# First mixer: the low part of each weight goes to VectorE or to GpSimd as a clock kept at build time tells

## The chip, the core and the metric

The kernel runs on one NeuronCore of a Trainium2 chip. The core's engines run side by side, each with its own queue of instructions: TensorE (PE in the profile; its weight loads are shown apart as PEld), VectorE (DVE), ScalarE (ACT), GpSimd (POOL) and SyncE (SP), which here only issues transfers. The metric is the device time of one execution in microseconds (us).

## The reference

Two transformer blocks run one after the other on 256 tokens of width 2048, all in float32. The change is in the first mixer of the first block:

```python
proj = h @ w_in[l]                                   # 8208 columns
o_hg  = hgrn2_group(proj[..., :HG_COLS], ...)        # q, f, v, g: 8 heads of 128
o_gdn = gdn_group(proj[..., HG_COLS:], ...)          # q, k, v through a causal convolution, gate, a, b
y = jnp.concatenate([o_hg, o_gdn], axis=-1) @ w_out[l]
x = x + gt_m * rmsnorm(y, post_mix_norm[l])
...
mod = silu(c) @ w_ada + b_ada                        # the shifts, scales and gates of a block
```

`hgrn2_group` and `gdn_group` are recurrences over chunks. The kernel turns each into a chain of small matrix products, exponentials, masks and products of elements.

## The kernel before

**Weights.** Every large weight is read once. It comes in units of 512 KB (128 partitions x 1024 values, tile `raw`), which SyncE loads into one of five buffers. A float32 product is made of three faster ones, so ScalarE rounds a unit to its high part (`wh<-raw`), and another engine makes the low part, which is the unit less its high part (`wl<-raw,wh`). TensorE then multiplies with both (`g<-hT,wh`, `g<-hT,wl`, or `g<-wh,hT`, as the block is laid out). There are four pairs of `wh` and `wl`. A raw buffer comes free for the next transfer once both parts are made. The other users of raw buffers are the units of the modulation, which VectorE multiplies and adds up (`acc<-raw,csil,acc`).

**Who makes the low part.** `l_eng` decides: an item marked `low` 3 goes to GpSimd if the build-time clock has it finished there no more than 3 us later than on VectorE, one marked otherwise goes to GpSimd if the mark is true and to VectorE if it is 0. Before, no weight of the first mixer has a mark. Those of the second mixer have, and there GpSimd makes 88 low parts.

**The build-time clock.** While the program is written out, `clk` runs a model of every engine (1.042 ns an element for a VectorE product, 2.2 ns for one on GpSimd). Each engine has its own time in it, and nothing in it couples VectorE with GpSimd. The order of instructions on every engine follows from this clock, and on the chip each engine keeps that order.

**The first mixer.** Its products run in 512-column blocks: `hq`, `hf`, `hv`, `hg`, (`ab`), `zq`, `zk`, `zv`, `gg` for the first half of the heads, and the same again for the second half; then `oA` and `oB`, the output projection. Three quarters of the first half's products run ahead of the stage. Between the products of a block, `fill` puts in steps of the chains, and makes the next units ready. The chains are generators (`hg_gen` of L1074, `gd_gen` of L1131, `head_out` of L1045):

- `hg_gen` has seven levels. On each, TensorE multiplies `hq,hk`, VectorE copies under a mask into `hgA` (COPY_PREDICATED) and updates `hq` and `hf`, and GpSimd updates `hk`. `head_out` then scales (`hgA<-hgA,rr,hg`), TensorE turns the result (`mx<-c,hgA`), and GpSimd makes its low part (`ol`). There are two of those, one for each half of the tokens.
- `gd_gen` inverts a triangular matrix in six levels. On each, TensorE multiplies `gdP,gdE`, ScalarE copies to `gdG`, TensorE multiplies `gdG,gdT`, VectorE subtracts from `gdP`, TensorE turns `gdP`. GpSimd masks `gdE`.
- The convolution (`zq`, `zk`, `zv`) is three multiply-adds of VectorE for each head. In the first half they read `part`, which is in SBUF; in the second half they read `g`, which is in PSUM.

Where a block's own follow-up is not done, the next one may not begin. `run` (L570) then takes steps of the chains, whichever the clock puts first, with no products between them:

```python
        while len(pri) > 1:
            clk.end = 0.0
            pri_step()
            if not clk.end:
                fill_step(True)
```

The case that matters is `hv` of the second half. Ahead of it, `ev_q` (L936) of the second half waits for the end of the first half's `hg_gen`:

```python
            while half and g.get("hg_done") != 0:
                yield
```

All engine instructions go through one helper, so the profile shows them under line 169; they are told apart by their tiles.

Of the kernel before, what the change touches and what calls it, by code (L numbers as in the profile page):

```python
# [178 lines left out]
def two_blocks(ctx, tc, I, out):  # L179
# [3 lines left out]
    pe, dve, act, pool, sync = (_Eng(clk, n, e) for n, e in (  # L183
        ("pe", nc.tensor), ("dve", nc.vector), ("act", nc.scalar), ("pool", nc.gpsimd), ("sync", nc.sync)))
# [45 lines left out]
    items = []  # L230
# [5 lines left out]
    def add_w(pieces, nk, n):  # L236
        items.append({"pieces": pieces, "nk": nk, "n": n})
        return len(items) - 1

    def add_ada(blk, vq, k, fin, row, cg):  # L240
        items.append({"ada": (blk, vq, k), "fin": fin, "row": row, "cg": cg})
# [46 lines left out]
    def prep(low=None):  # L288
# [14 lines left out]
        if "ada" in it:  # L303
            blk, vq, k = it["ada"]
            if it["cg"]:
                return ada_cg(it)
            a = st["accs", blk, vq]
            sc = csil[:, blk * 16 + k:blk * 16 + k + 1]
            if k == 0 and not it["row"]:
                dve.tensor_scalar(a, it["raw"], sc, None, op0=MUL)  # L310
            else:
                dve.scalar_tensor_tensor(a, it["raw"], sc, a, op0=MUL, op1=ADD)
            if it["fin"]:
                it["fin"]()
        else:
            n_ = it["nk"] * it["n"]
            it["slot"] = k, p = slots.popleft()
            h = p.tile([128, UK * 512], FR, name="wh", tag=f"wh{k}")
            l = p.tile([128, UK * 512], FR, name="wl", tag=f"wl{k}")
            act.activation(h[:, :n_], it["raw"][:, :n_], AF.Copy)  # L320
            if low is None:
                low = l_eng(it)
            low.tensor_tensor(l[:, :n_], it["raw"][:, :n_], h[:, :n_], op=SUB)
            held[k] = clk.key(h), clk.key(l)
            it["pe"] = 6 * n_ * 0.42e-3
            st["ahead"] += it["pe"]
            it["h"] = h[:, :n_].rearrange("p (k n) -> p k n", k=it["nk"])
            it["l"] = l[:, :n_].rearrange("p (k n) -> p k n", k=it["nk"])
# [36 lines left out]
    held = {}  # L365

    def l_eng(it):
        if it.get("low") != 3:
            return pool if it.get("low") else dve
        n = it["nk"] * it["n"]  # L370
        h = clk.t["act"]
        a = max(h, clk.t["dve"]) + 0.07 + n * 1.042e-3
        b = max(h, clk.t["pool"]) + 0.1 + n * 2.2e-3
        return pool if b <= a + 3.0 else dve

    def late_prep():
        i = st["p"]
        if i >= len(items) or "raw" not in items[i] or "ada" in items[i] or items[i].get("whole"):
            return False
        it = items[i]  # L380
        n = it["nk"] * it["n"]
        h = max(clk.t["act"], prep_at()) + 0.1 + n * 0.833e-3
        if it.get("low"):
            done = max(h, clk.t["pool"]) + 0.2 + n * 2.2e-3
        else:
            done = max(h, clk.t["dve"]) + 0.2 + n * 1.042e-3
        return done > clk.t["pe"] + st["ahead"] - lag[4]

    def prep_at():

        i = st["p"]
        if i >= len(items) or "raw" not in items[i]:
            return 0.0
        it = items[i]
        at = clk.wr[clk.key(it["raw"])][0]
        if "ada" not in it and slots:
            at = max([at] + [clk.rd.get(k, 0.0) for k in held.get(slots[0][0], ())])
        return at
# [57 lines left out]
    def fill(more=True):  # L456
        if pri:
            pri_step()
        fill_step(False, urgent)
        if more and late_prep():  # L460
            prep()
        for _ in range(2):
            if clk.t["dve"] - clk.t["pe"] > lag[1] or clk.t["act"] - clk.t["pe"] > lag[2] or not fill_step():
                break
        if more:
            for _ in range(2):
                if prep_at() > clk.t["pe"] + lag[3] or not prep():
                    break
# [1483 lines left out]
    def weight(k):  # L1952
        if k[0] in ("oB", "pB") or k == "fv" or k in (("f1", 0, 0), ("ga", 0, 0)) or k[:3] in (("f1", 0, 1), ("f2", 3, 2), ("f2", 3, 3)):
            return 0.0
        if k in ("qG", "kvH", "sv"):
            return 0.5
        if k == "ab" or k[1:] == (0,) and k[0] in ("hq", "hf", "hv", "hg", "zq", "zk", "zv", "gg"):
            return 0.0
        if k in (("hq", 1), ("hf", 1)):
            return 0.5  # L1960
        if k[0] == "oA":
            return 1.5
        return 1.0

    LOW = {k: 1 for k in ("qG", "kvH", "sv", "qA", "kB", "qC", "kD", "dv0", "dv1", "qE", "kF", "fdv")}
    LOW.update({k: 3 for k in LOW if isinstance(k, str)})
    for k in ("qG", "kvH"):
        del LOW[k]
    LOW.update({("pA", c): 2 for c in range(4)})
    ai = n_first  # L1970
    wide = [blocks[n, 0] for n in ("hq", "hf", "hv", "hg", "zq", "zk", "zv", "gg")]
    q_items = [ADA[q * 16:q * 16 + 16] for q in range(4)]
# [21 lines left out]
    for endkey, ntot in phases:  # L1994
        hi = order.index(endkey) + 1
        tot = sum(len(blocks[k].us) * weight(k) for k in order[lo:hi])
        tot = tot * 0.5 if endkey[0] == "up" else tot - (3 if endkey[0] == "pA" else 0 if endkey == "fdv" else 24)
        a0, na = ai, ntot - ai
        done = 0.0
        for k in order[lo:hi]:  # L2000
            b = blocks[k]
            b.idx = []
            for u in b.us:
                b.idx.append(add_w(*u))
                if k in (("f1", 0, 0), "fv", ("ga", 0, 0)):
                    items[-1]["whole"] = True
                items[-1]["low"] = k in LOW and (LOW[k] if LOW[k] == 3 else len(b.idx) % LOW[k] == 0)
                done += weight(k)
                while ai < ntot and (ai - a0) < na * done / tot:
                    for _ in range(1 + ADA[ai][5]):  # L2010
                        add_ada(*ADA[ai])
                        ai += 1
        lo = hi
# [65 lines left out]
    for b, o in zip(wide[1:], ("hk", "hv", "hg", "oh1", "ol1", "oh2", "ol2")):  # L2079
        a = g[o] if o in g else oTp.tile([128, 2, 512], F32, name="part", tag=o)  # L2080
# [140 lines left out]
    b = blocks["f2", 3, 3]  # L2221
# [97 lines left out]
    b = blocks["pB", 0]  # L2319
# [64 lines left out]
    b = blocks["dn", 2, 3]  # L2384
# [48 lines left out]
```

## Time and profile before

| what | value |
|---|---|
| time, median of 3 runs | 2723.72 us (2722.84 to 2728.7) |
| profiled execution: its own time | 2722.54 us |
| its span | 2720.8 us |
| TensorE busy | 2614.4 us (96%) |
| VectorE busy | 1823.5 us (67%) |
| ScalarE busy | 1261.0 us (46%) |
| GpSimd busy | 382.7 us (14%) |
| low parts on VectorE | 705, 871.2 us |
| low parts on GpSimd | 88, 206.0 us |

An engine's busy time is the sum of its instructions from start to end. An instruction that waits inside itself counts as busy for that long, so a busy share does not say how much work was done. Times below are counted from the start of the span. The first mixer, from where the second stage of its products begins, takes from 211 to about 740 us.

### The profile page before, as it was taken

What the parts mean: (1) busy time and instruction counts of PE and PEld (TensorE: products, weight loads), DVE (VectorE), ACT (ScalarE), POOL (GpSimd) and SP (SyncE); (2) the same over time, 40 slices, a digit from 0 to 9 for tenths busy, and PEclk for the clock granted to TensorE, in tenths of its full rate; (3) what the DMA queues carried; (4) which work ended last, traced back from release to release, by engine and by line L of the source; (5) the groups of instructions that cost most, each with busy time, mean ns of one, the idle gap of its engine ahead of it and who ended that gap; (6) DMA issues with size and microseconds to landing.
All of it is one profiled execution on the core that took longest, in us unless ns stands there. A gap on an engine that the chain in (4) does not pass through costs nothing.

```text
span 2720.8 us, 39596 instructions
## 1 busy us (share of the span) xinstructions
PE 2614.4 (96%) x15073; PEld 2198.1 (81%) x15073; DVE 1823.5 (67%) x2259; ACT 1261.0 (46%) x2124; POOL 382.7 (14%) x250
## 2 busy tenths in 40 slices
PE   7999889899999999999999999898999999999998
PEld 4788869768778888888886898796778888888886
DVE  3567978954678787887855465568767656655566
ACT  3434444344554454544544355454454444443443
POOL 1001142231000000000001155563400000000001
PEclk9999999999999999999999999998999999999999
DMA  9985968985579989989965865667677777666664
GB/s 361 318 262 148 239 194 219 264 251 184 174 252 302 319 284 303 318 291 325 311 192 165 233 205 179 210 220 243 212 232 244 244 244 219 196 191 192 188 186 147
DMA packets 399805, 643.58 MB, mean 237 GB/s; under 512 B 31480, under 2 KB 198088, under 8 KB 398208
## 3 DMA queue, kind: packets, MB, share of 16 engines
q1 hardware_dynamic: 391904, 627.03, 72.6%
q10 hardware_dynamic: 6960, 11.65, 1.2%
q8 instruction: 118, 1.93, 0.3%
q0 software_dynamic: 752, 2.39, 0.2%
q14 instruction: 71, 0.58, 0.1%
HBM read 636.27 MB, written 4.19 MB: 235 GB/s over the span
## 4 chain that ended last, share of the span: by engine, by line
PE 59%; DVE 4%; DMA 4%; issue 2%; ACT 2%; POOL 1%; SPq 0%; ACTq 0%; POOLq 0%; DVEq 0%
PE g L169 56%; PE mx L169 3%; DMA raw<-in_w_ff_dram 2%; DMA raw<-in_w_in_dram 1%; DVE wl L169 1%; ACT wh L169 1%; DVE acc L169 1%; DMA raw<-in_w_out_dram 1%; POOL wl L169 1%; DMA raw<-in_ada_w_dram 0%; DVE y L169 0%; DVE xres L169 0%; ACT S L169 0%; ACT sq L169 0%; DVE Sc L169 0%
## 5 line engine op out<-in xcount | busy, mean ns | idle before, releaser
L169 DVE TENSOR_TENSOR wl<-raw,wh 128x1024 fp32r<-128x1024 f32 x705 | 871.2, 1243 | 538.4 <-ACT wh L169 536.1
L169 ACT ACTIVATE wh<-raw 128x1024 fp32r<-128x1024 f32 (+2 forms) x793 | 823.5, 1045 | 880.1 <-PE g L169 391.7
L169 PE MATMUL g<-hT,wh 128*128 128x512 f32 (+1 forms) x4448 | 1212.1, 344 | 9.7 <-ACT wh L169 5.2
L169 PE MATMUL g<-hT,wl 128*128 128x256 f32 x3376 | 951.6, 282 | 8.7 <-DVE wl L169 5.8
L169 PEld LDWEIGHTS g<-hT,wh 128*128 128x128 f32 x4448 | 768.7, 190 | 125.5 <-issue 18.3
L169 PEld LDWEIGHTS g<-hT,wl 128*128 128x128 f32 x3376 | 641.4, 190 | 12.0 <-DVE wl L169 7.0
L169 DVE SCALAR_TENSOR_TENSOR acc<-raw,csil,acc 128x1024 f32<-128x1024 f32 x276 | 389.5, 1411 | 58.6 <-DMA raw<-in_ada_w_dram 57.4
L169 PE MATMUL g<-wh,rh 128*128 128x512 f32 x864 | 339.4, 393 | 0.0
L169 PE MATMUL g<-wh,rl 128*128 128x512 f32 x864 | 339.1, 393 | 0.0
L169 PE MATMUL g<-wl,rh 128*128 128x512 f32 x864 | 339.0, 392 | 0.0
L169 POOL TENSOR_TENSOR wl<-raw,wh 128x1024 fp32r<-128x1024 f32 (+2 forms) x88 | 206.0, 2354 | 232.5 <-ACT wh L169 218.8
L169 PEld LDWEIGHTS g<-wh,rh 128*128 128x128 f32 x864 | 162.6, 188 | 36.0
L169 PEld LDWEIGHTS g<-wh,rl 128*128 128x128 f32 x864 | 162.5, 188 | 36.1
L169 PEld LDWEIGHTS g<-wl,rh 128*128 128x128 f32 x864 | 162.7, 188 | 35.8
L169 PE MATMUL g<-wh,hT 128*128 128x512 f32 (+2 forms) x544 | 162.1, 369 | 2.1 <-ACT hq L169 1.8
L169 PEld LDWEIGHTS g<-wh,hT 128*128 128x128 f32 x544 | 97.9, 189 | 28.2 <-issue 12.6
L169 POOL TENSOR_TENSOR y<-yy,gw 128x512 f32<-128x512 f32 x6 | 7.7, 1301 | 697.2 <-DVE yy L169 697.2
L169 PE MATMUL g<-wl,hT 128*128 128x512 f32 (+2 forms) x272 | 98.4, 362 | 5.7 <-POOL wl L169 3.2
L169 PE MATMUL g<-raw,y 128*128 128x512 f32 (+1 forms) x192 | 84.2, 581 | 3.1 <-DVE y L169 2.9
L169 POOL TENSOR_TENSOR y<-y,gw 128x512 f32<-128x512 f32 x6 | 9.6, 1626 | 547.0 <-DVE y L169 541.5
L169 PE MATMUL ada<-raw,csil 128*32 128x512 f32 x384 | 63.8, 658 | 10.8 <-DMA raw<-in_w_ada_dram 9.3
L169 PEld LDWEIGHTS g<-raw,y 128*128 128x128 f32 x192 | 34.3, 190 | 38.1 <-issue 28.7
(453 smaller groups left out, 2569.7 us busy)
## 6 DMA issues: line engine op xcount, KB each, us to landing
raw<-in_w_ff_dram SPq DMA_DIRECT2D x256, 512.0 KB, 5.4
raw<-in_w_ada_dram SPq DMA_DIRECT2D x192, 512.0 KB, 5.7
raw<-in_ada_w_dram SPq DMA_DIRECT2D x192, 512.0 KB, 5.3
raw<-in_w_in_dram SPq DMA_DIRECT2D x176, 512.0 KB, 5.9
raw<-in_ffn_w_gate_dram SPq DMA_DIRECT2D x88, 512.0 KB, 4.6
raw<-in_ffn_w_up_dram SPq DMA_DIRECT2D x88, 512.0 KB, 4.7
raw<-in_ffn_w_down_dram SPq DMA_DIRECT2D x88, 512.0 KB, 4.4
raw<-in_w_out_dram SPq DMA_DIRECT2D x60, 512.0 KB, 4.8
```

Source lines behind the costliest of these rows:

```text
L169: r = f(out, *a, **kw)
```

## The change

Low parts of the first mixer get the mark 4: all blocks `hq` to `gg` from the point where the three early quarters are done, `ab`, and `oA`. Mark 4 means GpSimd if the build-time clock has it finished there no later than on VectorE, otherwise VectorE. `late_prep`, which decides whether a unit must be made ready at once, asks the same question. Nothing else is edited.

```diff
     def l_eng(it):
-        if it.get("low") != 3:
+        if it.get("low") not in (3, 4):
             return pool if it.get("low") else dve
         n = it["nk"] * it["n"]
         h = clk.t["act"]
         a = max(h, clk.t["dve"]) + 0.07 + n * 1.042e-3
         b = max(h, clk.t["pool"]) + 0.1 + n * 2.2e-3
-        return pool if b <= a + 3.0 else dve
+        return pool if b <= a + (3.0 if it["low"] == 3 else 0.0) else dve
...
-        if it.get("low"):
+        if it.get("low") and l_eng(it) is pool:
             done = max(h, clk.t["pool"]) + 0.2 + n * 2.2e-3
...
     LOW.update({("pA", c): 2 for c in range(4)})
+    LOW.update({(n, h): 4 for n in ("hq", "hf", "hv", "hg", "zq", "zk", "zv", "gg") for h in range(2)})
+    LOW.update({("oA", c): 4 for c in range(4)})
+    LOW["ab"] = 4
...
-                items[-1]["low"] = k in LOW and (LOW[k] if LOW[k] == 3 else len(b.idx) % LOW[k] == 0)
+                items[-1]["low"] = k in LOW and (LOW[k] if LOW[k] in (3, 4) else len(b.idx) % LOW[k] == 0)
```

In the program that comes out, GpSimd makes 118 low parts and VectorE 675, so 30 have moved. By their place among GpSimd's own instructions, 11 of them lie in the levels of the first `hg_gen` and its `head_out`, 2 in the first half's `gd_gen`, 12 in the second half's `hg_gen` and what stands beside it, and 5 in the second half's `gd_gen`. SyncE's order does not change.

On GpSimd, at the last levels of the first `hg_gen` (`hk` is the update of a level, `rr` and `ol` belong to `head_out`, `gdM` and `gdE` open `gd_gen`), the program before has:

```order
L169 TENSOR_TENSOR hk<-hk,hf 128x64x8
L169 TENSOR_TENSOR hk<-hk,hf 128x32x16
L169 TENSOR_TENSOR hk<-hk,hf 128x16x32
L169 TENSOR_TENSOR hk<-hk,hf 128x8x64
L169 TENSOR_TENSOR rr<-rr,mhalf 128x4
L169 TENSOR_TENSOR ol_3033<-hgA,oh_3032 128x4x128
L169 TENSOR_TENSOR rr<-rr,mhalf 128x4
L169 TENSOR_TENSOR ol_3033<-hgA,oh_3032 128x4x128
L169 TENSOR_TENSOR gdM_3309<-c_84,gla 128x512
```

and the changed one:

```order
L169 TENSOR_TENSOR hk<-hk,hf 128x64x8
L169 TENSOR_TENSOR wl<-raw,wh 128x1024 x2
L169 TENSOR_TENSOR hk<-hk,hf 128x32x16
L169 TENSOR_TENSOR wl<-raw,wh 128x1024
L169 TENSOR_TENSOR hk<-hk,hf 128x16x32
L169 TENSOR_TENSOR wl<-raw,wh 128x1024 x2
L169 TENSOR_TENSOR hk<-hk,hf 128x8x64
L169 TENSOR_TENSOR wl<-raw,wh 128x1024
L169 TENSOR_TENSOR rr<-rr,mhalf 128x4
L169 TENSOR_TENSOR wl<-raw,wh 128x1024 x3
L169 TENSOR_TENSOR ol_3006<-hgA,oh_3005 128x4x128
L169 TENSOR_TENSOR rr<-rr,mhalf 128x4
```

Nine of the eleven low parts of this place are in these rows (one stands ahead of them, one behind); `gdM` now comes after them.

On VectorE, at the last two of those levels, this is a piece of the difference:

```order
 L169 SCALAR_TENSOR_TENSOR acc<-raw,csil,acc 128x1024
-L169 TENSOR_TENSOR wl<-raw,wh 128x1024
 L169 COPY_PREDICATED hgA<-mk_1973,mx 128x4x64 x2
 L169 TENSOR_TENSOR hq<-hq,hf 128x8x64
 L169 TENSOR_TENSOR hf<-hf 128x8
 L169 SCALAR_TENSOR_TENSOR acc<-raw,csil,acc 128x1024
-L169 TENSOR_TENSOR wl<-raw,wh 128x1024
 L169 SCALAR_TENSOR_TENSOR zq<-part,cols,zq 128x253
```

The low parts are gone, and what stood around them stays. From the start of the stage to the second `hgA<-hgA,rr,hg`, VectorE has 23 low parts before and 13 after, and 13 and 14 `acc` steps.

On TensorE, where the products stop ahead of `hv` of the second half (`c_84` is the unit matrix, `g<-wh,hT` is the first product of `hv`), the program before has:

```order
L169 MATMUL mx<-c_84,hgA 128x128 x4
L169 MATMUL mx<-c_84,zk 128x128 x4
L169 MATMUL mx<-c_84,zq 128x128 x4
L169 MATMUL mx<-gdM_3309,c_84 128x512
L169 MATMUL mx<-gdE_3312,c_84 128x512
L169 MATMUL mx<-zk 128x128 x4
L169 MATMUL mx<-c_84,zk 128x128 x4
L169 MATMUL mx<-c_84,zv 128x128 x4
L169 MATMUL g<-wh,hT_176 128x512
```

and the changed one, from the turning of `zv` on (the rows ahead of it are the same but for `hgA`, which comes later):

```order
L169 MATMUL mx<-c_84,zv 128x128 x4
L169 MATMUL mx<-c_84,hgA 128x128 x4
L169 MATMUL mx<-c_84,gdT_3315 128x128 x4
L169 MATMUL mx<-gdP_3316,gdE_3317 128x64 x4
L169 MATMUL mx<-gdG_3312,gdT_3315 128x64 x4
L169 MATMUL mx<-c_84,gdP_3316 128x128 x4
L169 MATMUL mx<-gdP_3316,gdE_3317 128x64 x4
L169 MATMUL mx<-c_84,zq 128x128 x4
L169 MATMUL mx<-gdG_3312,gdT_3315 128x64 x4
L169 MATMUL mx<-c_84,gdP_3316 128x128 x4
L169 MATMUL mx<-gdP_3316,gdE_3317 128x64 x4
L169 MATMUL mx<-gdG_3312,gdT_3315 128x64 x4
```

Two more rows (`mx<-c_84,gdP` and `mx<-gdP,gdE`) follow before the first product of `hv`. So three levels of `gd_gen` and the start of a fourth, which before stood between products, now stand with no product between them.

## Rows read from the trace of the kernel before

**Rows 1.** Windows: us, busy PE, PEld, DVE, ACT, POOL; granted clock, DMA share, GB/s.

```profile
246.00:337.00 91.00, 83.03 (x663) 81.37 (x663) 86.99 (x140) 38.94 (x69) 18.18 (x10) 0.97 0.79 203
331.00:349.00 18.00, 9.03 (x35) 6.09 (x36) 9.37 (x20) 9.70 (x43) 11.66 (x10) 0.72 0.41 109
450.00:540.00 90.00, 79.92 (x638) 75.91 (x637) 84.04 (x123) 35.91 (x85) 23.06 (x16) 0.98 0.83 233
540.00:620.00 80.00, 73.53 (x444) 51.44 (x443) 39.84 (x71) 33.67 (x89) 29.22 (x24) 0.98 0.83 258
```

**Rows 2.** What TensorE waited for from 211 to 740 us.

```profile
PE g L169 <- DVE wl L169: 8.4, 7, 2.5
...
PE mx L169 <- DVE gdP L169: 4.0, 3, 2.1
```

**Rows 3.** VectorE's groups, 246 to 337: busy, mean ns | idle before.

```profile
L169 DVE TENSOR_TENSOR wl<-raw,wh 128x1024 fp32r<-128x1024 f32 x21 | 26.3, 1261 | 2.5 <-ACT wh L169 2.5
L169 DVE SCALAR_TENSOR_TENSOR acc<-raw,csil,acc 128x1024 f32<-128x1024 f32 x13 | 17.4, 1339 | 0.0
L169 DVE SCALAR_TENSOR_TENSOR zq<-part,cols,zq 128x255 f32<-128x255 f32 (+2 forms) x12 | 6.8, 564 | 0.3
L169 DVE COPY_PREDICATED hgA<-mk,mx 128x256 f32<-128x256 uint8 x14 | 6.6, 525 | 0.7 <-PE mx L169 0.6
L169 DVE TENSOR_TENSOR hq<-hq,hf 128x512 f32<-128x512 f32 x7 | 6.0, 856 | 0.0
L169 DVE SCALAR_TENSOR_TENSOR zv<-part,cols,zv 128x255 f32<-128x255 f32 (+2 forms) x12 | 5.7, 478 | 0.1
...
L169 DVE TENSOR_TENSOR part<-g,part 128x512 f32<-128x512 f32 x8 | 5.1, 679 | 0.0
```

**Rows 4.** VectorE's groups, 760 to 1480, where GpSimd is nearly idle.

```profile
L169 DVE TENSOR_TENSOR wl<-raw,wh 128x1024 fp32r<-128x1024 f32 x248 | 301.1, 1225 | 124.9 <-ACT wh L169 124.0
L169 DVE SCALAR_TENSOR_TENSOR acc<-raw,csil,acc 128x1024 f32<-128x1024 f32 x122 | 156.1, 1279 | 0.9 <-DMA raw<-in_ada_w_dram 0.4 <-DMA raw<-in_w_ada_dram 0.2
```

**Rows 5.** Instructions in time (start, length): VectorE and GpSimd, mostly second mixer.

```profile
306.08 0.68 DVE L169 TENSOR_TENSOR hq<-hq,hf 128x512 f32<-128x512 f32 x1
504.71 1.06 POOL L169 TENSOR_TENSOR hk<-hk,hf 128x512 f32<-128x512 f32 x1 [6.98 <-PE mx L169]
1606.01 2.39 POOL L169 TENSOR_TENSOR wl<-raw,wh 128x1024 fp32r<-128x1024 f32 x1 [1.76 <-ACT wh L169]
1606.18 2.37 DVE L169 TENSOR_TENSOR Sc<-Sc,cs 128x128 f32<-128x128 f32 x1
1608.78 0.29 DVE L169 TENSOR_TENSOR Sc<-Sc,cs 128x128 f32<-128x128 f32 x1
1610.90 2.37 POOL L169 TENSOR_TENSOR wl<-raw,wh 128x1024 fp32r<-128x1024 f32 x1 [2.50 <-ACT wh L169]
1611.77 1.95 DVE L169 SCALAR_TENSOR_TENSOR S<-cb,mx 128x384 f32<-128x384 f32 x4 [1.50 <-PE mx L169]
1616.68 1.94 DVE L169 SCALAR_TENSOR_TENSOR S<-cb,mx 128x384 f32<-128x384 f32 x4
```

**Rows 6.** TensorE in time around the stop ahead of `hv`.

```profile
336.07 1.17 PE L169 MATMUL mx<-c,hgA 128*128 128x128 f32 x4 [5.45 <-DVE hgA L169]
...
348.37 0.50 PE L169 MATMUL g<-wh,hT 128*128 128x512 f32 x1 [1.77 <-ACT hq L169]
...
357.73 0.50 PE L169 MATMUL g<-wl,hT 128*128 128x512 f32 x1 [2.50 <-DVE wl L169]
```

**Rows 7.** The steps of one level of `gd_gen`, in time.

```profile
408.36 1.00 PE L169 MATMUL mx<-gdP,gdE 128*128 128x64 f32 x8
409.46 0.39 ACT L169 ACTIVATE gdG<-mx 128x256 f32<-128x256 f32 x1 [0.30 <-PE mx L169]
410.15 0.41 DVE L169 TENSOR_TENSOR gdP<-gdP,mx 128x256 f32<-128x256 f32 x1
410.71 0.63 PE L169 MATMUL mx<-c,gdP 128*128 128x128 f32 x4
```

## The prediction

> **What bounds the kernel now.** I read the page first: TensorE is busy for 96% of the span, so outside the mixers there is little to win or to lose, and the change edits only the first mixer. Then the busy time by stretches, and the reader is to see where VectorE is full [rows 1]. From 246 to 337 it is busy for 86.99 of 91 us, from 450 to 540 for 84.04 of 90; from 540 to 620 for only 39.84 of 80. These full stretches are where it could be worth taking work off VectorE. Then TensorE's waits: from 211 to 740 it waits 8.4 us for low parts of VectorE and 4.0 us for `gdP` [rows 2]. In time, its longest wait is 5.45 us, for the scaled `hgA` of VectorE, at 336.07, where all products of the first half are done and those of `hv` may not begin before 348.37 [rows 6]. VectorE is thus what this stretch waits for at its end: whatever makes VectorE later at 336 makes TensorE later by as much. GpSimd is far from full there (18.18 of 91 us).
>
> **What the change removes and adds on VectorE.** A low part takes VectorE 1.225 us where GpSimd is quiet [rows 4] and 1.261 us in the first full stretch [rows 3]. On GpSimd it takes 2.37 us when it runs unhindered [rows 5]. Were the two engines independent, the 30 moves would relieve VectorE of 30 x 1.225 = 37 us and load GpSimd with 71 us that it has to spare.
>
> They are not independent. At 1606.01 GpSimd starts a low part of 2.39 us; at 1606.18 VectorE starts a product with both inputs in SBUF, which takes 2.37 us; the same instruction takes 0.29 us at 1608.78, with GpSimd idle [rows 5]. It stood still until GpSimd was done. During the next low part, at 1610.90, VectorE runs four multiply-adds with one input from PSUM, and these take 1.95 us, against 1.94 at 1616.68 with GpSimd idle [rows 5]: they are not held. So a low part on GpSimd holds back every VectorE instruction that has two inputs in SBUF, for as long as it lasts. It costs VectorE f x 2.37 us, where f is the share of GpSimd's time that falls on such instructions, against 1.225 us saved. At f = 0.52 that is nothing won.
>
> The Trainium skill says this in "SBUF — State Buffer", section "Who interferes with whom": VectorE and GpSimd share a port pair by an exclusive lock held for the whole instruction, and a VectorE instruction with two SBUF inputs contends with a GpSimd instruction that reads SBUF. The trace agrees (2.37 us for 0.29). If every GpSimd low part blocked VectorE for its whole length, as the page's rule would have it on a saturated VectorE, f would be 1, and the sum below would come to about 2758 us; that case is a rival below, from rows.
>
> **First stretch (246 to 337): +8.6 us.** What is f here? Below: in the stretch before, the held instructions can be seen in their means. Low parts are 0.036 us longer than undisturbed (x21), `acc` 0.060 (1.339 against 1.279, x13), `zq<-part` 0.086 longer than the like `zv<-part` (x12), `hq` 0.18 longer than the 0.68 of 306.08 (x7) [rows 3 to 5]: 0.8 + 0.8 + 1.0 + 1.2 = 3.8 us, for GpSimd's seven `hk` at 1.06 us and two smaller instructions that I set at one `hk` each, some 9.5 us. That is f = 0.4, a lower bound, since smaller groups are left out. Above: 1. By the mix: of 87 us only `COPY_PREDICATED` (6.6) and `part<-g,part` (5.1) read PSUM [rows 3], so (87.0 - 11.7) / 91 = 0.83 of the time VectorE is in something that can be held. I take 0.75. Up to the second scaling of `hgA`, VectorE loses ten low parts (10 x 1.225 = 12.2 us) and gains one `acc` (1.3 us): -11.0 us. The eleven low parts of GpSimd give back 11 x 2.37 x 0.75 = +19.6 us. The net is +8.6 us (f = 0.4: -0.6; f = 1: +15.1), and as TensorE already waits for this instruction, it arrives there in full.
>
> **The stop ahead of `hv`: +8 us.** The new order puts three and a half levels of `gd_gen` into the stop. One level is 1.00 + 0.39 + 1.00 + 0.41 + 0.63 = 3.4 us of work in sequence (its second product has the shape of the first) [rows 7], plus four hand-overs of 0.15 us (410.15 + 0.41 to 410.71): 4.0 us, of which TensorE works 2.6 and stands for 1.4. Before them come the mask, the subtraction and the copy that make `gdT` and `gdP`, which before were covered by products from 348.37 on: five instructions of 0.4 to 1.1 us each, as the like ones of [rows 5, 7], with a hand-over each, which I estimate at 5 us. The three and a half levels add 3.5 x 1.4 = 4.9. From that go the 2.50 us that TensorE waited at 357.73 in the same time [rows 6]. That makes 7.4 us; the granted clock, 0.72 from 331 to 349 (a mean of its two levels, 1.2 and 2.4 GHz, where TensorE was half idle) [rows 1], will stay low for longer, so I take 8. Below: 4, if the steps before the levels overlap with the turning of `hgA`. Above: 12, if the roughly 10 us of TensorE's work in the longer stop run at 0.72.
>
> **After it: -2 us.** With the levels done, the 4.0 us of waits for `gdP` [rows 2] fall in part: -2 (0 to -4). Only two low parts move there.
>
> **Second full stretch (450 to 540): +1 us.** Twelve low parts move. VectorE saves 14.7 us. More of its work there reads PSUM (the convolution of the second half), so I take f = 0.55: 12 x 2.37 x 0.55 = 15.6, a net of +1 us. Bounds: f = 0.4 gives -3.3, f = 1 gives +13.7. From 540 on, VectorE is half idle [rows 1] and five moves are hidden by its slack: 0; without that slack each would cost 2.37 - 1.225 = 1.1 us.
>
> What is queued behind a low part on GpSimd is the next `hk` or `gdE`, which TensorE needs for the next level; the waits for products that come before them are long, and I give this nothing. Raw buffers are freed 1.1 us later for a moved unit, hidden by the other four. The transfers stay in the same order.
>
> **Sum.** 8.6 + 8 - 2 + 1 + 0 = 15.6 us. On the profiled execution's 2722.54 us that is 2738.1; the median of the runs shown is 1.2 us above it, so 2739 us.
>
> **The rivals.**
> *Full hold (0.18).* VectorE is held for the whole of each low part, f = 1: 15.1 + 8 - 2 + 13.7 = 34.8 us, 2758.5 us. For it: the row at 1606.18. Against: PSUM instructions slip through, and where VectorE runs back to back GpSimd may wait instead, which costs VectorE nothing.
> *Faster (0.18).* GpSimd mostly finds gaps, f stays below 0.42, where the first stretch breaks even (11.0 / 26.1). Then TensorE's wait of 5.45 us at the stop goes, about 5 of the 8.4 us of waits for low parts [rows 2] go, and the waits for `gdP` give 2; the longer stop costs 4: -8.5 us, 2715 us. For it: the 0.4 seen with short `hk`, and that the clock's new order would then hold. Against: VectorE has only 4 us of idle time in that stretch.
> *No change (0.14).* f near 0.5, the stop at its lower bound, the waits for `gdP` all gone: 2 + 4 - 4 - 1 = +1 us, 2725 us.
> The forecast, from 2729 to 2750 us, has 0.50.
>
> **How the numbers follow.** A difference below 0.2% (5.4 us) is about what a measurement of this kernel can't tell from no change. Slower by more: the forecast and the full hold, 0.68. Within: 0.14. Faster by more: 0.18. The range reaches from 2714 (half of the faster case lies below) to 2757 (more than half of the full hold lies above), which leaves out about 0.2. The likeliest case's own range is 2729 to 2750.
>
> **What would show it.** In the changed kernel's trace, 30 low parts on GpSimd from 246 to 720 us, at 2.4 us or more each. In the first full stretch the means of VectorE's `acc` and `zq<-part` rise well above 1.34 and 0.56 us, and those of `COPY_PREDICATED` and `part` do not. The turning of `zk` that now opens the stop begins later than 337 by about 9 us, and the first product of `hv` later than 348.4 by some 25 us or more, of which a part is made up later. From 760 us on nothing differs but the offset. I am wrong if `acc` keeps its mean (then nothing is held), if the first product of `hv` comes by 360 us, or if the offset arises after 450 us, from waits of TensorE for low parts of GpSimd.

## The result, and the profile after

The changed kernel takes 2766.49 us (median of 4 runs, 2761.59 to 2767.98), the kernel before 2726.21 us beside it (2722.84 to 2732.45): a ratio of 1.0138, with an interval of 1.0125 to 1.0152. By this ratio it is slower by about 38 us, where 15.6 were forecast, and it lies above the range. The profiled execution took 2761.59 us, its span is 2759.8 us.

The page's groups of low parts in the changed kernel (busy us, mean ns | idle before): the 30 moves are there.

```profile
L169 DVE TENSOR_TENSOR wl<-raw,wh 128x1024 fp32r<-128x1024 f32 (+1 forms) x675 | 837.2, 1248 | 539.7 <-ACT wh L169 531.6
...
L169 POOL TENSOR_TENSOR wl<-raw,wh 128x1024 fp32r<-128x1024 f32 (+2 forms) x118 | 282.8, 2404 | 296.5 <-ACT wh L169 276.9
```

VectorE's and GpSimd's groups in the first full stretch of the changed kernel, which lasts from 246 to 346 us here:

```profile
L169 DVE SCALAR_TENSOR_TENSOR acc<-raw,csil,acc 128x1024 f32<-128x1024 f32 x13 | 20.9, 1605 | 0.0
L169 DVE TENSOR_TENSOR wl<-raw,wh 128x1024 fp32r<-128x1024 f32 x11 | 14.4, 1307 | 3.5 <-ACT wh L169 3.5
L169 DVE TENSOR_TENSOR hq<-hq,hf 128x512 f32<-128x512 f32 x7 | 13.1, 1877 | 0.0
L169 DVE SCALAR_TENSOR_TENSOR zk<-part,cols,zk 128x255 f32<-128x255 f32 (+2 forms) x12 | 11.7, 975 | 0.1
L169 DVE SCALAR_TENSOR_TENSOR zq<-part,cols,zq 128x255 f32<-128x255 f32 (+2 forms) x12 | 10.9, 907 | 0.2
L169 DVE SCALAR_TENSOR_TENSOR zv<-part,cols,zv 128x255 f32<-128x255 f32 (+2 forms) x12 | 7.3, 608 | 0.1
L169 DVE COPY_PREDICATED hgA<-mk,mx 128x256 f32<-128x256 uint8 x14 | 6.6, 521 | 0.7 <-PE mx L169 0.6
...
L169 POOL TENSOR_TENSOR wl<-raw,wh 128x1024 fp32r<-128x1024 f32 x10 | 26.8, 2682 | 25.6 <-ACT wh L169 23.6 <-DVE acc L169 2.0
```

Against [rows 3], the large groups with two SBUF inputs are longer (`acc` 1605 ns for 1339, `hq` 1877 for 856, `zq` 907 for 564; low parts least, 1307 for 1261), and the copy that reads PSUM is not (521 for 525). Instructions in time show one such place, and what TensorE makes of it:

```profile
286.64 2.50 POOL L169 TENSOR_TENSOR wl<-raw,wh 128x1024 fp32r<-128x1024 f32 x1 [7.13 <-ACT wh L169]
286.79 3.89 DVE L169 SCALAR_TENSOR_TENSOR zk<-part,cols,zk 128x255 f32<-128x255 f32 x2
289.09 1.31 POOL L169 TENSOR_TENSOR hk<-hk,hf 128x512 f32<-128x512 f32 x1
290.36 2.56 POOL L169 TENSOR_TENSOR wl<-raw,wh 128x1024 fp32r<-128x1024 f32 x1
290.60 3.41 DVE L169 SCALAR_TENSOR_TENSOR acc<-raw,csil,acc 128x1024 f32<-128x1024 f32 x1
293.93 0.74 DVE L169 COPY_PREDICATED hgA<-mk,mx 128x256 f32<-128x256 uint8 x2
294.59 0.68 DVE L169 TENSOR_TENSOR hq<-hq,hf 128x512 f32<-128x512 f32 x1
295.19 0.20 DVE L169 TENSOR_TENSOR hf<-hf 128x32 f32<-128x32 f32 x1
...
295.42 1.94 PE L169 MATMUL mx<-hq,hk 128*128 128x64 f32 x8 [3.12 <-DVE hf L169]
```

Two `zk` steps need 3.89 us and one `acc` 3.41 us, where about 0.96 and 1.28 us are usual. The `zk` steps end 0.28 us after GpSimd's `hk` (290.40), and `acc`, which began 0.24 us after the low part beside it, ends 1.09 us after that (292.92). `COPY_PREDICATED`, `hq` and `hf` are queued behind them, and TensorE waits 3.12 us for that `hf`.

TensorE in time around the stop ahead of `hv` (start, length, idle before), with two GpSimd rows:

```profile
343.76 0.28 PE L169 MATMUL g<-hT,wl 128*128 128x256 f32 x1
...
346.26 0.44 PE L169 MATMUL mx<-c,zk 128*128 128x128 f32 x2 [2.00 <-DVE zk L169]
...
349.57 2.34 POOL L169 TENSOR_TENSOR wl<-raw,wh 128x1024 fp32r<-128x1024 f32 x1 [4.30 <-ACT wh L169]
...
351.87 2.02 POOL L169 TENSOR_TENSOR gdM<-c,gla 128x512 f32<-128x512 f32 x1
...
353.94 2.07 PE L169 MATMUL mx<-gdM,c 128*128 128x512 f32 x2 [6.81 <-POOL gdM L169]
...
361.62 0.66 PE L169 MATMUL mx<-c,hgA 128*128 128x128 f32 x4 [1.28 <-ACT kz L169]
...
364.85 1.12 PE L169 MATMUL mx<-c,gdT 128*128 128x128 f32 x4 [2.57 <-DVE gdT L169]
366.74 1.94 PE L169 MATMUL mx<-gdP,gdE 128*128 128x64 f32 x8 [0.78 <-ACT gdP L169]
...
387.53 0.77 PE L169 MATMUL g<-wh,hT 128*128 128x512 f32 x1
```

The turning of `zk` stood at 337.03 before, 0.96 us behind the row of `hgA` in [rows 6], so this stop begins 9.2 us later. The first half's last product, the first row above, starts 13.4 us later than the one before it did:

```profile
330.34 0.28 PE L169 MATMUL g<-hT,wl 128*128 128x256 f32 x1
```

The first product of `hv` comes 39.2 us later than in [rows 6]. A step of a level takes 1.94 us for the 1.00 of [rows 7]. The windows:

```profile
246.00:346.00 100.00, 86.97 (x663) 84.06 (x662) 94.98 (x125) 39.16 (x69) 41.52 (x20) 0.95 0.69 174
...
350.00:390.00 40.00, 26.93 (x106) 22.52 (x107) 13.71 (x21) 13.41 (x48) 20.23 (x17) 0.54 0.17 56
...
450.00:540.00 90.00, 81.80 (x575) 78.12 (x574) 80.84 (x98) 31.52 (x80) 42.24 (x20) 0.91 0.81 223
```

In the stop the granted clock is 0.54, close to the lower of its two levels, the transfers are at 0.17, and VectorE has work for 13.71 of 40 us. The same 40 us of the kernel before:

```profile
350.00:390.00 40.00, 34.98 (x183) 28.44 (x182) 28.54 (x39) 18.71 (x47) 12.82 (x10) 0.96 0.71 211
```

There VectorE is busy for 28.54 us, and the clock is 0.96. What TensorE waited for from 211 to 740 us, to be held against [rows 2]:

```profile
PE mx L169 <- DVE gdP L169: 9.6, 7, 2.3
PE mx L169 <- DVE hf L169: 8.6, 4, 3.7
PE mx L169 <- POOL gdM L169: 6.8, 1, 6.8
PE mx L169 <- DVE hgA L169: 5.3, 3, 2.0
```

The waits for low parts of VectorE are no longer among the large ones. In their place TensorE waits for the chains: `hf`, `hgA` and `gdP` of VectorE, `gdM` of GpSimd.

### The profile page after: what moved, and what is told of

The parts are those of the page before. It is cut to its first block, busy times and chain, and to the rows that moved or that the text cites. A ratio compares the mean times of both kernels' runs of the same rounds, so it can differ in the third digit from the quotient of the medians.

```text
span 2759.8 us, 39611 instructions
## 1 busy us (share of the span) xinstructions
PE 2636.2 (96%) x15073; PEld 2214.5 (80%) x15073; DVE 1837.2 (67%) x2229; ACT 1260.7 (46%) x2124; POOL 453.3 (16%) x280
## 4 chain that ended last, share of the span: by engine, by line
PE 55%; DMA 6%; DVE 5%; ACT 3%; issue 2%; POOL 1%; SPq 0%; ACTq 0%; POOLq 0%; DVEq 0%
PE g L169 53%; DMA raw<-in_w_ff_dram 3%; PE mx L169 3%; DVE wl L169 2%; ACT wh L169 1%; DMA raw<-in_w_in_dram 1%; DVE acc L169 1%; POOL wl L169 1%; DMA raw<-in_w_out_dram 1%; DMA raw<-in_ada_w_dram 1%; ACT S L169 0%; DVE y L169 0%; DMA xres<-xspill 0%; DVE xres L169 0%; SPq L169 0%
## 5 line engine op out<-in xcount | busy, mean ns | idle before, releaser
L169 DVE TENSOR_TENSOR wl<-raw,wh 128x1024 fp32r<-128x1024 f32 (+1 forms) x675 | 837.2, 1248 | 539.7 <-ACT wh L169 531.6
L169 DVE SCALAR_TENSOR_TENSOR acc<-raw,csil,acc 128x1024 f32<-128x1024 f32 x276 | 399.0, 1446 | 52.1 <-DMA raw<-in_ada_w_dram 47.1
L169 POOL TENSOR_TENSOR wl<-raw,wh 128x1024 fp32r<-128x1024 f32 (+2 forms) x118 | 282.8, 2404 | 296.5 <-ACT wh L169 276.9
L169 PEld LDWEIGHTS g<-wh,hT 128*128 128x128 f32 x544 | 97.6, 189 | 24.1 <-issue 10.5
```

What stands on the lines that cost most here:

```text
L169: r = f(out, *a, **kw)
```

## The experiments

Fourteen kernels were run. The ratio is to the kernel before on the same chip, with its 95% interval; that kernel's medians were 2726.2 to 2728.7 us. The columns behind it follow TensorE, in us later than in the kernel before. "hv" is the start of the first product of `hv` behind the stop, read from the timeline (348.37 in the kernel before). For the others the columns of its products into `g` are counted in the trace, and the time at which the same count is reached is taken less that of the kernel before, as a mean over the stretch in which the kernel before runs from 323 to 330 us (end of the first half's products), 445 to 457, and 590 to 610 us.

| run | ratio | interval | 323 | hv | 445 | 590 |
|---|---|---|---|---|---|---|
| the change | 1.0138 | 1.0125 to 1.0152 | 14.9 | 39.2 | 31.0 | 38.4 |
| order alone | 1.0040 | 1.0026 to 1.0054 | 5.6 | 27.7 | 16.8 | 14.7 |
| engine alone | 1.0077 | 1.0062 to 1.0092 | 6.6 | 10.2 | 15.4 | 21.0 |
| first eleven moves | 1.0102 | 1.0087 to 1.0117 | 15.4 | 37.7 | 26.9 | 30.2 |
| other nineteen | 1.0044 | 1.0029 to 1.0059 | 0.3 | 0.2 | 6.3 | 14.0 |
| change, no levels in the stop | 1.0097 | 1.0080 to 1.0114 | 16.5 | 17.1 | 23.9 | 30.9 |
| engine alone, filled | 0.9992 | 0.9982 to 1.0001 | | | | |
| before, earlier end mark | 0.9983 | 0.9974 to 0.9992 | 0.1 | -8.8 | -3.4 | -1.4 |
| order alone, four fills a step | 1.0072 | 1.0058 to 1.0086 | 8.7 | 34.2 | 22.5 | 20.2 |
| change, filled | 1.0030 | 1.0019 to 1.0041 | 1.6 | 24.6 | 10.5 | 6.4 |
| order alone, two fills a level step | 1.0063 | 1.0046 to 1.0080 | 8.3 | 30.4 | 18.0 | 14.3 |
| last five moves | 1.0007 | 0.9996 to 1.0018 | 0.2 | 0.0 | 1.1 | 0.8 |
| engine alone, in quarters | 1.0085 | 1.0067 to 1.0103 | 5.1 | 9.0 | 8.9 | 18.3 |
| order alone, filled waits | 1.0046 | 1.0031 to 1.0062 | 5.2 | 30.3 | 19.8 | 16.0 |
| earlier end mark, filled wait | 1.0005 | 0.9994 to 1.0016 | 0.7 | -8.5 | -4.4 | -1.1 |

One profile each stands behind these columns. Where the order of the products differs, the offset moves by up to 4 us within a stretch, so two or three microseconds in them mean little. For the filled engine alone no columns are given: its profiled execution took 4749.75 us and can't be set beside the others.

**Order and engine apart.** The first two runs split the change in two. The order alone keeps the clock's choice but issues on VectorE:

```diff
-            low.tensor_tensor(l[:, :n_], it["raw"][:, :n_], h[:, :n_], op=SUB)
+            if low is pool and it["low"] == 4:
+                nc.vector.tensor_tensor(l[:, :n_], it["raw"][:, :n_], h[:, :n_], op=SUB)
+                clk.run("pool", "tensor_tensor", l[:, :n_], [it["raw"][:, :n_], h[:, :n_]], [])
...
```

> The changed kernel's order on every engine, but the 30 moved low parts are issued on VectorE at the same places, so nothing new runs on GpSimd. Theory 1 (a low part on GpSimd holds VectorE back, and this carries the loss): nearly all of the loss goes, 2726 to 2731 us; acc in the first full stretch stays near 1.34 us. Theory 2 (the new order carries it: the levels of gd_gen in the stop ahead of hv, at a low clock): most of the loss stays, 2750 us or more. My reading of the two traces has both: no hold before the stop (13 us less), the longer stop (+26) and what is made up after it (-13) stay, nothing in the second half: 2739 us, with 2734 to 2746 as its range; the first product of hv about 374 us from the span's start.

The engine alone takes the kernel before and issues the same 30 units on GpSimd, while the clock is told VectorE:

```diff
+            if i in MOVED:
+                nc.gpsimd.tensor_tensor(l[:, :n_], it["raw"][:, :n_], h[:, :n_], op=SUB)
+                clk.run("dve", "tensor_tensor", l[:, :n_], [it["raw"][:, :n_], h[:, :n_]], [])
...
```

> The order of the kernel before on TensorE, ScalarE and SyncE; the same 30 units have their low part issued on GpSimd. Theory 1 (hold): the first stretch loses about 13 us and the second about 12, 2750 us (2742 to 2758), acc in the first stretch at 1.6 us or more, and the stop starts about 9 us later but is as long as before. Theory 2 (order): 2726 to 2731 us. Were the two engines independent, some waits for low parts would go and the time would fall to 2715 to 2722 us.

They took 2740.67 and 2750.13 us: neither theory alone. Order 0.40% and engine 0.77% make 1.17% of the 1.38%; what is left, 0.21%, is no more than the three intervals allow. In the engine alone, TensorE and VectorE's groups from 246 to 346 us show the hold without any new order:

```profile
346.13 1.17 PE L169 MATMUL mx<-c,hgA 128*128 128x128 f32 x4 [8.86 <-DVE hgA L169]
...
358.57 0.51 PE L169 MATMUL g<-wh,hT 128*128 128x512 f32 x1 [1.77 <-ACT hq L169]
```

```profile
L169 DVE SCALAR_TENSOR_TENSOR acc<-raw,csil,acc 128x1024 f32<-128x1024 f32 x13 | 20.6, 1584 | 0.0
L169 DVE TENSOR_TENSOR wl<-raw,wh 128x1024 fp32r<-128x1024 f32 x11 | 18.7, 1697 | 3.4 <-ACT wh L169 3.4
```

The turning of `hgA` comes 10.1 us later than in [rows 6], the first product of `hv` 10.2 us: the stop keeps its length. In the order alone the stop begins 0.95 us earlier than before (336.08 for 337.03) and still lasts until 376.06:

```profile
336.08 0.44 PE L169 MATMUL mx<-c,zk 128*128 128x128 f32 x2 [1.06 <-DVE zk L169]
...
353.43 1.09 PE L169 MATMUL mx<-c,gdT 128*128 128x128 f32 x4 [6.22 <-DVE rk L169]
...
360.30 1.12 PE L169 MATMUL mx<-c,gdP 128*128 128x128 f32 x4 [0.58 <-DVE gdP L169]
...
376.06 0.77 PE L169 MATMUL g<-wh,hT 128*128 128x512 f32 x1
```

**The moves by place.** Marks are kept on the first eleven units, or on the other nineteen:

```diff
+                if items[-1]["low"] == 4 and len(items) - 1 > 162:
+                    items[-1]["low"] = 0
```

> The changed kernel with only its first 11 moves (those of the first full stretch), with its order up to and through the stop ahead of hv; all later low parts on VectorE. By the two traces: 13 us lost before the stop, 26 in it, 13 made up behind it, so +26: 2752 us (2745 to 2758), and by 450 us the offset is final. If the second half carries the loss instead (what the stop loses is made up in full): 2735 us or less.

> Only the other 19 moves (2 in the first half's gd_gen, 12 beside the second hg_gen, 5 behind it), with the order of the kernel before up to and through the stop ahead of hv. By the two traces the second full stretch loses 10 to 15 us: 2738 us (2733 to 2743). If VectorE's share held there is the 0.55 that I had predicted, the loss is 1 us: 2724 to 2730 us.

They took 2756.88 and 2741.38 us, both 3 to 5 us above the point of the expectation and within its range; their 1.02% and 0.44% make 1.46%, so the change is about the sum of its places. The first eleven lose 37.7 us up to the first product of `hv`, and 10.8 us of it are made up by 445. The nineteen lose 6.3 us up to 445, where two moves lie, and 7.7 us more in the second full stretch. The 0.55 forecast for that stretch would have given 1 us.

**The last five alone**, in the order of the kernel before:

```diff
+RAW_BUFS, HL_BUFS = 5, 4; MOVED = {273, 279, 282, 291, 300}
```

> Order of the kernel before, and only the five low parts from about 540 us on are issued on GpSimd. The forecast gave these 0, because VectorE is half idle there: 2726 to 2730 us. Without cover they would cost 1.1 us each: 2732 to 2735 us.

2728.41 us, no difference: that term of the forecast holds.

**Does GpSimd's reading hold VectorE, or is it GpSimd's queue?** GpSimd is kept as long, but fills the tile in place of reading; the 30 low parts are missing from the result. First in the order of the kernel before (shown against the engine alone), then in the changed order:

```diff
-                nc.gpsimd.tensor_tensor(l[:, :n_], it["raw"][:, :n_], h[:, :n_], op=SUB)
+                nc.gpsimd.tensor_tensor(l[:, :8], it["raw"][:, :8], h[:, :8], op=SUB)
+                nc.gpsimd.memset(l[:, 8:n_].bitcast(F32), 0.0)
+                nc.gpsimd.memset(l[:, 8:n_].bitcast(F32), 0.0)
+                nc.gpsimd.memset(l[:, 8:n_ // 2].bitcast(F32), 0.0)
```

> As the run with the engine alone changed (order of before, 30 low parts on GpSimd), but GpSimd computes only the first 8 columns of each and then fills the tile with zeros, two and a half times over, so that it is busy for about 2.4 us without reading SBUF; the 30 low parts are left out of the result. Theory 1 (VectorE is held by GpSimd's reads): the 22 us of loss go, 2718 to 2730 us, acc in the first stretch at 1.35 us or less. Theory 3 (GpSimd's own queue: hk, gdE, gdM and the products wait behind long low parts): the loss stays, 2742 to 2750 us.

> The changed kernel with its order, but GpSimd computes only the first 8 columns of each of the 30 low parts and fills the tile with zeros for the rest of about 2.4 us (the 30 low parts are left out of the result). VectorE is relieved and not held. Theory 1 (hold) with theory 2 (the longer stop): no worse than the order alone, 2728 to 2741 us. Theory 3 (gdM, hk and ol late in GpSimd's own queue): 2745 us or more, with TensorE waiting for gdM by 5 us or more in the stop.

2726.65 and 2733.18 us: the engine's 0.77% goes to nothing, and the change's 1.38% to 0.30%. Nor is there a gain: with 30 low parts (37 us) off VectorE, nothing held and the old order, the time stays the same. Why relief alone wins nothing is open, since that run has no trace to set beside the others. In the changed order with fills, from 246 to 346 us:

```profile
L169 DVE SCALAR_TENSOR_TENSOR acc<-raw,csil,acc 128x1024 f32<-128x1024 f32 x15 | 19.2, 1277 | 0.4 <-DMA raw<-in_w_ada_dram 0.4
...
L169 DVE TENSOR_TENSOR hq<-hq,hf 128x512 f32<-128x512 f32 x7 | 6.6, 940 | 0.0
...
L326 POOL MEMSET wl<- 128x1016 f32 x11 | 10.4, 947 | 0.6
L325 POOL MEMSET wl<- 128x1016 f32 x11 | 10.4, 945 | 0.0
```

`acc` is back at 1277 ns while GpSimd is as busy as with the low parts. The Trainium skill, "SBUF — State Buffer", section "Who interferes with whom", says that a VectorE instruction with two SBUF inputs does not contend with a GpSimd instruction that only writes; the trace agrees. The wait for `gdM` in the stop stays, at 5.7 us, in a kernel that loses only 0.30%. So the hold is what the low parts on GpSimd cost, and GpSimd's own queue costs little.

**The same GpSimd work in quarters** (engine alone):

```diff
+                for c in range(4):
+                    s = slice(c * n_ // 4, (c + 1) * n_ // 4)
+                    nc.gpsimd.tensor_tensor(l[:, s], it["raw"][:, s], h[:, s], op=SUB)
```

> As the run with the engine alone changed, but each of the 30 low parts is issued on GpSimd as four instructions of 256 columns. If the hold lasts as long as one GpSimd instruction and VectorE gets its turn between two of them, VectorE loses less: 2734 to 2743 us. If it goes by GpSimd's whole time: 2747 to 2754 us.

2747.48 us, as with whole low parts. GpSimd's group from 246 to 346 us:

```profile
L326 POOL TENSOR_TENSOR wl<-raw,wh 128x256 fp32r<-128x256 f32 x40 | 39.3, 1012 | 22.8 <-ACT wh L169 20.4 <-ACT geg L169 2.4
```

Four quarters take 4.05 us where one whole took 2.86 in the engine alone, so GpSimd is busy for longer. VectorE's `acc` there has a mean of 1503 ns, against 1584 in the engine alone and 1339 before: it is held less, but still held. Why the time is no better is not settled.

**The stop ahead of `hv`.** The mark that ends `hg_gen` was set in a step of its own, which the clock puts behind `ol` on GpSimd; with low parts ahead of `ol`, levels of `gd_gen` came first. The edit sets it one step earlier, in the changed kernel and in the kernel before:

```diff
             yield from head_out(A[:, tl].rearrange("p a b -> p (a b)"), p, None, sg[:, tl], hgw, dst, tl)
-            yield
+            if not tl:
+                yield
         g["hg_done"] = half
```

> The changed kernel, but the first half's hg_gen sets its end mark in the step that issues its last turning and no longer in a step of its own, which the clock puts behind the end of ol on GpSimd. The stop ahead of hv then ends at that turning, and all levels of gd_gen lie between products. Theory 2 (the levels in the stop carry 14 us net: 27 in the stop less 13 made up): 2752 us (2746 to 2758), first product of hv by about 370 us instead of 387.5. Rival (the levels cost as much between products as in the stop): 2762 to 2768 us.

> The kernel before with the edit of the end mark alone (nothing moved to GpSimd): the stop ahead of hv ends at the last turning of hg_gen, and the steps that open gd_gen lie between products. If a stop costs its length less what is made up: 3 to 6 us faster, 2721 to 2725 us. If the chains then end later by as much: 2726 to 2730 us.

2756.24 and 2723.69 us. Without levels in the stop the changed kernel's first product of `hv` comes at 365.49 us, 22 us earlier, and 0.41% (11 us) of that stays to the end. The kernel before with the edit is 0.17% faster, below the 0.2% that the prediction takes as no change, and of the 8.8 us won at the stop 1.4 are left at 590.

**The low clock in the stop.** In the order alone the granted clock is 0.50, its lower level, from 350 to 380 us, where TensorE runs dependent steps with waits between them. Products whose result is overwritten were added, four ahead of every TensorE step of the stop, then two ahead of the levels' steps, then 8 and 24 in the long waits and one ahead of a step; the last run puts 20 into the wait for `hgA` of the kernel before with the earlier mark. The edit, as the last two have it:

```diff
-        return ps["m"].tile([128, 512], F32, name="mx", tag="mx")
+        p = ps["m"].tile([128, 512], F32, name="mx", tag="mx")
+        for _ in range(fill if st.get("warm") else 0):
+            nc.tensor.matmul(p[:, 0:128], ident, ident, start=True, stop=True, skip_group_check=True)
+        return p
```

> As the run with the order alone (changed order, no low part moved to GpSimd), with four products of 128 columns, whose result is overwritten, ahead of each TensorE step of the stop ahead of hv. If the low granted clock is what makes the stop long (0.50 there, and TensorE's steps take twice their time): the clock stays above 0.8, and the stop becomes 5 to 10 us shorter in spite of the added work: 2731 to 2736 us. If the stop is made of other engines' steps and hand-overs: the added products only cost, 2741 to 2748 us.

> The order alone, with only two added products ahead of each TensorE step of the levels in the stop, none ahead of the steps before them. By the rows of the order alone, TensorE's steps from 353 to 377 us take 18.7 us at the clock of 0.50 where the same steps take 10.0 at full clock, so 8.7 us of the stop are the clock. If the added products keep it up and mostly lie in waits: 4 to 7 us faster than the order alone, 2734 to 2737 us. If they cost what they win, as four ahead of every step did: 2739 to 2743 us.

> The order alone, with the added products put where TensorE waits longest in the stop: 8 ahead of gdE's product (a wait of 3.1 us), 24 ahead of the turning of gdT (6.2 us), and one ahead of each step of the levels (0.5 to 0.8 us). At full clock one takes about 0.22 us, so they fit into the waits. If the clock of 0.50 is a price of the stop (8.7 us by the rows): granted clock above 0.9 from 345 to 378, the levels from the turning of gdT to the first product of hv take 17 to 19 us instead of 25.3, and the whole 2732 to 2736 us. If the levels are as long at full clock, other engines' steps set them, and the time stays at 2738 to 2743 us.

> The kernel before with the end mark set a step earlier (0.9983 of the kernel before when run alone), and 20 added products ahead of the last turning of hgA, where TensorE waits 5.65 us. The turning and the products behind it then run at full clock instead of half: about 2 us less in the stop. If that holds to the end: 0.997 to 0.998 of the kernel before (2719 to 2722 us). If VectorE and the transfers set the end of the stretch up to 540 us, it is given back: 0.998 to 0.9995.

2748.38, 2741.93 and 2741.14 us, against 2740.67 without fills; and 2729.34 us. None gave the gain that was hoped for. The second and third lie in the range for no gain, the first just above it, and the fourth misses both of its ranges. At 590 us the fourth stands where the earlier mark alone stands (-1.1 and -1.4), so in the traces the difference between those two (0.22%) arises behind it, where their programs are the same, and can't be put to the fills. The third, in time:

```profile
358.77 0.60 PE L169 MATMUL mx<-c,gdT 128*128 128x128 f32 x4
...
363.43 0.65 PE L169 MATMUL mx<-c,gdP 128*128 128x128 f32 x4 [0.31 <-DVE gdP L169]
```

Here the first level takes 4.66 us (358.77 to 363.43), against 6.87 in the order alone (353.43 to 360.30), and up to the first product of `hv` (378.64) it is 19.9 us, against 22.6. (The 25.3 us of the expectation counted to a later row.) So the low clock does lengthen the levels. But `gdT` was ready at 353.99 and the 24 fills ran on to 358.93, so its turning came 5.3 us later than in the order alone, and from 370 to 380 the clock was at 0.53 again. What the stop would cost at full clock stays open.

## Why the prediction was wrong

**Hold: right in kind; that its size fits at the stop is in part luck.** Against undisturbed lengths ([rows 3 to 5]; `zv` of [rows 3] for the three convolutions) VectorE loses 13 x 0.326 on `acc`, 7 x 1.197 on `hq`, 11 x 0.082 on low parts, 12 x 0.497 on `zk`, 12 x 0.429 on `zq` and 12 x 0.130 on `zv`: 26.2 us, less the 3.8 that were there before, 22.4 us for 26.8 us of low parts on GpSimd. That is a share of 0.84. The forecast's 0.75 was of 2.37 us a low part, and of 10 x 2.37 us the 22.4 are 0.95. The stop begins 9.2 us later, forecast 8.6, but not by the path that I gave, a longer wait for `hgA`. TensorE is 13.4 us late when the first half's last product starts, after waits such as that for `hf`, and of that the order alone has 4.2 (334.52 for 330.34). The 5.45 us that it stood for `hgA` before are gone, because in the new order `hgA` is turned only at 361.62. My path shows in the engine alone, where that wait is 8.86 us and the stop begins 10.1 us later.

**The stop: this step failed.** I put the longer stop at +8 and what follows it at -2, together +6. The change is at +9.2 when the stop begins and at +31.0 by 445: +21.8. With the order alone it is from -1.0 to +16.8: +17.8, so most of it needs no hold. Two terms were too small. The levels there took 22.6 us (353.43 to 376.06), where three and a half at 4.0 us make 14; TensorE's twelve steps of 353 to 377 take 18.7 us at half clock and would take about 10.0 at the lengths of [rows 7]: 8.7 us, and I had 0.6 us for the clock. The waits before them (3.1 and 6.2 us in the order alone) were 9.3 us, estimated at 5. With both put right the +6 becomes +18.4, an estimate, near the +17.8. The engine alone loses a further 5.2 us from the first product of `hv` to 445, where I gave the hold of the few low parts that move there nothing.

How much is made up? These rows run from the first product of `hv` to the count of columns that the kernel before reaches at 451 us: the kernel before, the order alone, the change, the change with fills.

```profile
348.40:451.00 102.60, 95.29 (x608) 83.21 (x609) 82.98 (x102) 46.81 (x110) 26.87 (x19) 0.98 0.83 236
376.11:468.24 92.13, 88.39 (x545) 76.33 (x545) 69.72 (x89) 43.45 (x103) 24.34 (x14) 0.98 0.83 223
387.58:482.45 94.87, 88.00 (x545) 75.59 (x546) 71.45 (x85) 43.55 (x103) 31.97 (x18) 0.99 0.80 214
373.04:461.96 88.92, 86.99 (x545) 75.93 (x545) 65.72 (x85) 43.30 (x103) 32.43 (x26) 0.99 0.86 230
```

The order alone needs 10.5 us less than the kernel before. Of these, 6.9 us are TensorE's work, 63 records that the stop had already done; I had rightly not priced that work. Only 3.6 us are waits saved, and there were only 7.3 us of waits to save (102.60 less 95.29). So what TensorE loses in the stop by standing and by the half clock mostly stays lost, because it has little idle time behind it. VectorE stands still in the stop too (13.71 us of work in 40 us, for 28.54 before), but it is not full behind it, 69.72 of 92.13 us. That it has some part is supported by the change with fills, in which VectorE has 30 low parts less to make and is not held: TensorE's waits fall to 1.9 us there, and of 24.6 us at the first product of `hv` 6.4 are left at 590, in the order alone 14.7 of 27.7. The earlier mark in the kernel before fits as well (8.8 us won, 1.4 kept): the work that leaves the stop must be done between products.

**Second full stretch: failed too.** Forecast +1, measured +7.4 (31.0 to 38.4); the nineteen moves alone show 6.3 to 14.0. The hold is there: in the change VectorE's `acc` has a mean of 1663 ns from 450 to 540, for 1427 before. TensorE's row for the same products, up to the count that the kernel before reaches at 600 us, before and in the change:

```profile
451.00:600.00 149.00, 132.45 (x930) 110.10 (x931) 117.20 (x181) 60.84 (x156) 46.12 (x34) 0.98 0.84 244
482.45:638.76 156.31, 137.67 (x919) 114.98 (x919) 125.15 (x165) 58.84 (x145) 70.03 (x44) 0.93 0.85 243
```

Of 7.3 us more, 5.2 are in TensorE's busy time, at a granted clock of 0.93 for 0.98, and 2.1 in its waits. My sum had no term for the clock there. Order alone gains 2.1 us in this stretch and engine alone loses 5.6, 3.5 together. Why the change loses more is not shown. What I argue is that the clock kept at build time, which knows no hold, sets the levels of `hg_gen` as if VectorE were free, and that TensorE then meets held steps; but in the order alone, with no low part of the first mixer on GpSimd, it also waits for `hq` and `hf` there, 6.7 us from 450 to 540. I had said that waits for low parts of GpSimd after 450 would prove me wrong; the offset does arise there in part, but TensorE waits for no low part of GpSimd.

**Right:** 0 from 540 on (last five moves); `COPY_PREDICATED` and `part` unheld; the first product of `hv` 25 us or more later; GpSimd's queue given nothing (the wait for `gdM` is 6.8 us, but the change with fills keeps 5.7 of it and loses 0.30%).

**The sum.** Hold was forecast at 8.6 + 1 = 9.6 us and is 21 us when alone (0.77%); order at 6 and is 11 (0.40%). The full hold, 2758.5 us, was too low as well: its held share was nearer to the 0.95, but it left the stop as it was.

## What to carry to other kernels

An engine's saved time is worth nothing if the taker holds it back: try an offload with the taker kept busy in a way that can't hold (a fill of the same length), which shows the most that it could win (here nothing), and with the new order but the old engine, and the two prices come apart. A planner whose clock knows no coupling between two engines also moves everything that waits for them, so read the new order first for chain steps that land in a stop. Price a stop by all that the fullest engine, here TensorE, loses in it, its slower steps at the low clock included; behind the stop it gets back only the idle time that it still has there (7.3 us here).

## What the hardware showed that I had not expected

One SBUF input can be enough to be held: in the changed kernel `rk<-ssk`, a TENSOR_SCALAR of 128x4, ends with GpSimd's `gdM` (351.87 + 2.02) after 1.00 us, where its like takes 0.15. The same holds in that stop for `rk<-rk`, `rq<-rq` and `sv<-s`, of the same form, which end within 0.04 us of GpSimd's `gdM`, `gdG` and `gdH`.

```profile
352.92 1.00 DVE L169 TENSOR_SCALAR rk<-ssk 128x4 f32<-128x4 f32 x1
...
356.80 0.15 DVE L169 TENSOR_SCALAR rq<-ssq 128x4 f32<-128x4 f32 x1
```

The same section of the Trainium skill, "SBUF — State Buffer", has VectorE instructions in a two-port mode contend with GpSimd too, and names `tensor_scalar` among those that can enter it; this row agrees, and my rule of two inputs was too narrow. Splitting did not help the time either: a quarter low part on GpSimd takes 1.01 us, 4.05 for four, and the kernel lost as much, though VectorE was held somewhat less.
